# An encoder layer on one core: weight-block sums for w_o and four feed-forward groups moved from VectorE to accumulating DRAM transfers

## The chip, the cores and the metric

The kernel runs on one core of one Trainium2 chip. The metric is device time in microseconds of one execution. The kernel before took 1222.36 us, the median of three runs (1221.72 to 1222.45). One further execution was recorded by the hardware profiler; all trace times are counted from the start of its span.

## What is computed

One layer of an encoder, batch 1, 1024 positions, 1024 channels, fp32 throughout. The reference, cut to what matters here:

```python
mod = jax.nn.silu(c) @ w_ada + b_ada
sh1, sc1, gt1, sh2, sc2, gt2 = jnp.split(mod[:, None, :], N_MOD, axis=-1)

h = rmsnorm(x, norm1_g) * (1.0 + sc1) + sh1
z = h @ w_in
u, v, q, k, va, gate_a, gate_b = jnp.split(z, cuts, axis=-1)
a_out = gmlp_branch(u, v, gm_v_g, gm_w_s, gm_b_s) @ w_a
b_out = window_attention_branch(q, k, va, q_norm_g, k_norm_g, attn_sink) @ w_b
merged = jax.nn.sigmoid(gate_a) * a_out + jax.nn.sigmoid(gate_b) * b_out
x = x + gt1 * (merged @ w_o)

h2 = rmsnorm(x, norm2_g) * (1.0 + sc2) + sh2
f_gate, f_up = jnp.split(h2 @ w_ffn_in, 2, axis=-1)
x = x + gt2 * ((jax.nn.silu(f_gate) * f_up) @ w_ffn_out)
```

`w_ffn_in` is split into `w_gate` and `w_up`, 1024 x 2816 each, handled in 22 groups of 128 columns.

## The kernel before

**Precision.** Every fp32 operand is split into a high part (a copy to float32r) and a low part (operand minus high part). A product is three matrix multiplications: high x high, high x low, low x high. The high part is made on ScalarE (ACT), the low part mostly on VectorE (DVE), so each weight tile of 128 x 1024 costs one ACT copy and one DVE subtraction before TensorE (PE) may use it.

**Stages.** The positions are handled in two halves of 512. For each half: q, k, v, windowed attention and the gating branch, two branch projections. Then, over all 1024 positions, the gates (`gate_products`), the output projection (`out_products`), the feed-forward up and gate projections, and the down projection.

**Seven products instead of eight.** From the gates on, a product over two halves of the positions and two blocks of weight rows is done as a 2 x 2 block product by Winograd's scheme: seven block products, with sums of weight blocks and of activation blocks in place of the eighth. With weight blocks a11, a12, a21, a22 the sums are

- w1 = a21 + a22
- S = a11 + w1
- al = a12 + S
- w2 = a11 + a21

In a feed-forward group f, a11 and a12 are the two 512-column halves of `w_gate[f]`, a21 and a22 those of `w_up[f]`. Four *units* of weights are split for each group: unit 0 is the raw gate block, unit 1 is S beside w1, unit 2 is al beside w2, unit 3 is a22 alone. `STEPS` lists the seven products by unit, half and activation block. For w_o, the blocks of pair p are the halves of `w_o[2p]` and `w_o[2p+1]`, four pairs in all.

**Where the sums are made.** For w_o: during attention of the second half, `merged_sums` loads a pair into one `mid` tile (two loads of 512 KB on SyncE's queue, SP), four DVE additions make the sums in place, and one store of 1 MB on GpSimd's queue (POOL) writes them to the DRAM tile `sO`. `out_products` later loads parts of `sO` into `raw` tiles (`need`, kinds A and C). For the feed-forward groups: `prep(f, u, part)` does them while PE works; for unit 1 and for unit 2 two DVE sums each fill the tile `ws`, then part 0 makes the high part and part 1 the low part. In the kernel before, unit 1 holds -S, and the activation block T2 that it meets is plain.

**Order.** PE, ACT and DVE run in program order, written out by hand in the gates and in the feed-forward part (`in_order`, `manual_schedule`); `out_products` is ordered by a small planner, `Plan`, from costs and due times. SP issues nearly all loads, in order, and a load that waits for its buffer holds back those behind it. POOL issues the stores: `md` and `pd` (branch products, for the gates), `x1d` (the residual rows after w_o, read back by SP a little later), `tA`, `tB`, `wS`. POOL also computes the inverse square roots (`rcol`), which PE waits for through `spread`.

**The gates.** `gate_products` runs over six groups d = 2 to 7, each 84 multiplications of 128x512. Within a group: after the first product `gate_sums(d, 2)` makes sums on DVE and then issues the load of `gb` for group d + 1; after the fourth product `gate_sums(d + 1, 1)` reads it. At the end of a group `load_p` loads the four `pd` tiles of the next. In the first group, after its sixth product, two loads of `md` (512 KB each) are issued on POOL.

**Buffers.** `raw` and the split weights `wh`, `wl` have three buffers each, `mid` eight. The feed-forward part loads a gate block three groups ahead (`load_gate`), an up block two groups ahead (`load_up`, two buffers), and the fourth block of group 0 by itself into the `ss` tile. `run_chain` works off the list of activation blocks (`t1_sum`, `t2_sum`, `low`, ...) beside the first products; each entry is one or two instructions.

Of the kernel before, what the change touches and what calls it, by code (L numbers as in the profile page):

```python
# [16 lines left out]
P = 128  # L17
# [17 lines left out]
FA, FB, FC = 2, 1, 4  # L35
PLAIN_GATES = 2
ZEROS = (9, 1)
BIAS = 4
# [69 lines left out]
def kernel(  # L108
# [209 lines left out]
    tB = dram.tile([NP, P, 4 * HALF], F32, tag="tB", name="tB")  # L318
    sO = dram.tile([KT // 2, P, 4 * HALF], F32, tag="sO", name="sO")


# [251 lines left out]
    def open_ffn():  # L573
# [3 lines left out]
        fps.append(fp)  # L577

    def merged_sums(p):

        t = mid.tile([P, 2048], F32, tag="mid", name=nm("wo"))
        for i in range(2):
            load(t[:, i * UNIT : (i + 1) * UNIT], w_o[2 * p + i])
        a11, a12, a21, a22 = (t[:, i * HALF : (i + 1) * HALF] for i in range(4))
        ops = [(a22, a21, a22), (a21, a11, a21), (a11, a22, a11), (a12, a11, a12)]

        def one(n):
            out, a, b = ops[n]
            V.tensor_tensor(out, a, b, op=ALU.add)
            if n == 3:  # L590
                store(sO[p], t)
        return one

# [49 lines left out]
    def half(hf):  # L643
# [416 lines left out]

        pts = None
        pair_sums = [merged_sums(0)] if hf else []
        adds = 0
        for s in range(nw):
# [5 lines left out]
            if hf == 0:  # L1070
                if s % 2 == 0:
                    ada_load()
                if s:
                    ada_late(*ada_loaded.pop(0), silu_c)
                if s == nw - 1:
                    ada_late(*ada_loaded.pop(0), silu_c)
            else:
                if s % 2 == 0 and s < nw - 2:
                    pair_sums.append(merged_sums(s // 2 + 1))
                for _ in range((0, 3, 3, 2, 2, 2, 2, 2)[s]):  # L1080
                    pair_sums[adds // 4](adds % 4)
                    adds += 1
            fill(FA)
# [76 lines left out]
        for d in range(KT):  # L1160
# [24 lines left out]
            for j, (o, br) in enumerate(((512, (oH, oL)), (0, (gH, gL)))):  # L1185
# [9 lines left out]
                if d < PLAIN_GATES:  # L1195
                    sg = sgs.pop(0)
                    V.scalar_tensor_tensor(out=sg, in0=sg, scalar=1.0, in1=pb, op0=ALU.add, op1=ALU.mult)
                    ms.append(sg)
                else:
                    p = tmp()  # L1200
                    A.copy(p, pb)
                    store(pd[hf, d, 1 - j], p)
            if d < PLAIN_GATES:
# [181 lines left out]
    def gate_products(hH, hL):  # L1385
# [14 lines left out]
        def merge(s, p):  # L1400
            V.scalar_tensor_tensor(out=s, in0=s, scalar=1.0, in1=p, op0=ALU.add, op1=ALU.mult)

        run_tokens(99)
        tokens.extend(tokens_late)
        run_tokens(4)
        ps = load_p(GD[0])
        for d in GD:
            banks = {}
            for i, (u, part, t, b, first) in enumerate(STEPS):
# [382 lines left out]

    RG, RU, U = {}, {}, {}
    a22 = []

# [11 lines left out]
    def load_up(f):  # L1807
        if f < NF:
            RU[f] = ups[f % 2]
            dma(RU[f], w_up[f])  # L1810

    def prep(f, u, part):

        g, r = RG[f], RU.get(f)
        if part == 0:
            if u == 1:
                V.tensor_tensor(ws[:, Q:], r[:, :Q], r[:, Q:], op=ALU.add)
                V.scalar_tensor_tensor(out=ws[:, :Q], in0=ws[:, Q:], scalar=-1.0, in1=g[:, :Q],
                                       op0=ALU.mult, op1=ALU.subtract)
            elif u == 2:  # L1820
                V.tensor_tensor(ws[:, Q:], g[:, :Q], r[:, :Q], op=ALU.add)
                V.tensor_tensor(ws[:, :Q], g[:, Q:], ws[:, :Q], op=ALU.subtract)
            U[f, u] = wtiles(UNIT if u < 3 else Q)
            A.copy(U[f, u][0], (g, ws, ws, a22[0] if f == 0 else r[:, Q:])[u])
            return
        h, l = U[f, u]
        V.tensor_tensor(l, (g, ws, ws, a22[0] if f == 0 else r[:, Q:])[u], h.bitcast(F32), op=ALU.subtract)
        if u == 2:
            load_gate(f + 3)
        if u == 3 and f or (f, u) == (0, 2):  # L1830
            load_up(f + 2)
# [123 lines left out]
    def chain_12(rb):  # L1955
        for k in range(4):
# [3 lines left out]
            if k:  # L1960
                chain.append(lambda k=k: low(X0[:, k - 1, :], T2, k - 1))
            chain.append(lambda k=k: low(X0[:, k, :], T1, k))
            chain.append(lambda k=k: t2_sum(k))
        chain.append(lambda: low(X0[:, 3, :], T2, 3))

# [81 lines left out]
    with tc.manual_schedule():  # L2047
        U[4, 0], U[5, 0], U[0, 0], U[1, 0] = early
        buf = mid.tile([P, 2048], F32, tag="mid", name=nm("ws"))
        ws, ups = buf[:, :UNIT], (buf[:, UNIT:], fp.tile([P, UNIT], F32, tag="ru", name="ru"))  # L2050
        load_up(0)
        load_up(1)
        g3 = gate_raw(3)
        load_gate(0)
        product(0, 0)
        U[2, 0] = wtiles()
        split2(raw2[0], *U[2, 0])
        evict(0, 0)
        load_gate(1)
        product(0, 1)  # L2060
# [259 lines left out]
```

## Time and profile before

| what | us |
|---|---|
| median of three runs | 1222.36 |
| the profiled execution | 1221.94 |
| its span, first to last instruction | 1220.2 |
| PE busy | 1211.0 |
| DVE busy | 928.5 |
| ACT busy | 582.4 |
| POOL busy | 150.6 |

The granted TensorE clock is full throughout (1.00). Attention of the second half lies around 270 to 345 us of the span, the gates around 387 to 501, the output projection around 501 to 575, and the first feed-forward groups follow.

A row of the page's groups reads: line, engine, operation, out<-in by the program's names, shapes, count, then busy us, mean ns of one, idle time of the engine just before and what ended it. Nearly all compute instructions are recorded through one helper and carry its line, L145, so the tile names tell them apart. A row of the timeline reads: start us, duration, engine, line, operation, tiles, count, and in brackets the idle time before it and its releaser. A row of transfers gives count, KB of each and the median us from issue to landing. The view of waits reads: who waited for whom, us in total, times, longest. SPq is the issuing of transfers by SyncE.

### The profile page before, as it was taken

What the parts mean: (1) busy time and instruction counts of PE and PEld (TensorE: products, weight loads), DVE (VectorE), ACT (ScalarE), POOL (GpSimd) and SP (SyncE); (2) the same over time, 40 slices, a digit from 0 to 9 for tenths busy, and PEclk for the clock granted to TensorE, in tenths of its full rate; (3) what the DMA queues carried; (4) which work ended last, traced back from release to release, by engine and by line L of the source; (5) the groups of instructions that cost most, each with busy time, mean ns of one, the idle gap of its engine ahead of it and who ended that gap; (6) DMA issues with size and microseconds to landing.
All of it is one profiled execution on the core that took longest, in us unless ns stands there. A gap on an engine that the chain in (4) does not pass through costs nothing.

```text
span 1220.2 us, 15626 instructions
## 1 busy us (share of the span) xinstructions
PE 1211.0 (99%) x5653; PEld 1007.2 (83%) x5653; DVE 928.5 (76%) x1504; ACT 582.4 (48%) x954; POOL 150.6 (12%) x182
## 2 busy tenths in 40 slices
PE   9999999999999999999999999999999999999998
PEld 7888888888888888877888888888888888888887
DVE  8999977789978776897997767675676766765646
ACT  5667865367855443644553333333333334433341
POOL 0024323024322000001100001000000000000001
PEclk9999999999999999999999999999999999999999
DMA  9752169653277233477313446455555449995552
GB/s 363 284 180 99 35 217 358 248 216 134 104 259 240 96 117 103 148 233 266 103 49 122 172 157 223 173 192 187 190 190 199 163 155 372 394 354 190 190 172 104
DMA packets 78096, 236.54 MB, mean 194 GB/s; under 512 B 8898, under 2 KB 9154, under 8 KB 72772
## 3 DMA queue, kind: packets, MB, share of 16 engines
q1 hardware_dynamic: 63028, 163.20, 38.6%
q0 software_dynamic: 14992, 72.36, 15.8%
q8 instruction: 44, 0.72, 0.3%
q14 instruction: 32, 0.26, 0.1%
HBM read 176.28 MB, written 59.24 MB: 193 GB/s over the span
## 4 chain that ended last, share of the span: by engine, by line
PE 93%; DVE 4%; issue 1%; DMA 1%; ACT 1%; POOL 0%; SPq 0%; DVEq 0%; ACTq 0%; POOLq 0%
PE mm L145 47%; PE at L145 46%; DVE mid L145 2%; DMA raw<-in_w_q_dram 1%; DVE wl L145 1%; DMA mid<-in_xA_dram 0%; DVE ss L145 0%; DVE h L145 0%; DVE ws L145 0%; ACT wh L145 0%; DVE t L145 0%; DVE tt1l L145 0%; ACT mid L145 0%; ACT h L145 0%; DVE b22l L145 0%
## 5 line engine op out<-in xcount | busy, mean ns | idle before, releaser
L145 DVE TENSOR_TENSOR wl<-raw,wh 128x1024 fp32r<-128x1024 f32 (+1 forms) x135 | 159.0, 1182 | 61.7 <-ACT wh L145 61.1
L145 ACT CAST wh<-raw 128x1024 fp32r<-128x1024 f32 (+1 forms) x149 | 152.2, 1023 | 112.1 <-PE mm L145 39.9
L145 PE MATMUL mm<-mid,wh 128*128 128x512 f32 x640 | 197.7, 390 | 0.8 <-DVE mid L145 0.8
L145 PEld LDWEIGHTS mm<-mid,wh 128*128 128x128 f32 x640 | 119.8, 188 | 25.8 <-DVE mid L145 1.2
L145 PE MATMUL mm<-wh,h 128*128 128x512 f32 x384 | 124.7, 397 | 0.5 <-ACT h L145 0.5
L145 PE MATMUL mm<-mid,wl 128*128 128x512 f32 x320 | 124.7, 390 | 0.0
L145 PE MATMUL mm<-h,wh 128*128 128x512 f32 x304 | 94.4, 392 | 0.0
L145 PE MATMUL at<-h,wh 128*128 128x512 f32 x304 | 93.9, 390 | 0.0
L145 PEld LDWEIGHTS mm<-wh,h 128*128 128x128 f32 x384 | 70.8, 188 | 14.2 <-ACT h L145 0.9
L145 DVE TENSOR_TENSOR wl<-ws,wh 128x1024 fp32r<-128x1024 f32 (+1 forms) x54 | 60.8, 1125 | 24.2 <-ACT wh L145 24.1
L145 ACT CAST wh<-ws 128x1024 fp32r<-128x1024 f32 (+1 forms) x54 | 52.5, 973 | 42.9 <-DVE ws L145 28.0
L145 PE MATMUL mm<-wl,h 128*128 128x512 f32 x192 | 71.2, 391 | 0.0
L145 PEld LDWEIGHTS mm<-mid,wl 128*128 128x128 f32 x320 | 60.1, 188 | 12.6
L145 PEld LDWEIGHTS at<-h,wh 128*128 128x128 f32 x304 | 56.9, 188 | 11.7
L145 PEld LDWEIGHTS mm<-h,wh 128*128 128x128 f32 x304 | 56.6, 188 | 11.6
L145 ACT ACTIVATE t<-t 128x512 f32<-128x512 f32 x46 | 28.4, 631 | 71.2 <-DVE t L145 71.2
L145 DVE TENSOR_TENSOR ol<-raw,oh 128x1024 fp32r<-128x1024 f32 x30 | 36.6, 1224 | 31.4 <-ACT oh L145 29.8
L145 PE MATMUL mm<-h,wl 128*128 128x512 f32 x152 | 59.4, 391 | 0.0
L145 PE MATMUL at<-h,wl 128*128 128x512 f32 x152 | 59.3, 390 | 0.0
L145 ACT ACTIVATE xs<-xs 128x512 f32<-128x512 f32 x21 | 13.3, 632 | 94.5 <-DVE xs L145 94.5
L145 ACT CAST oh<-raw 128x1024 fp32r<-128x1024 f32 x30 | 31.6, 1053 | 44.8 <-PE at L145 21.5
L145 PE MATMUL at<-wl,wh 128*128 128x512 f32 (+1 forms) x136 | 52.7, 388 | 0.0
(296 smaller groups left out, 2882.0 us busy)
## 6 DMA issues: line engine op xcount, KB each, us to landing
mid<-in_w_ada_dram SPq DMA_DIRECT2D x28, 512.0 KB, 8.3
raw<-in_w_gate_dram SPq DMA_DIRECT2D x28, 512.0 KB, 3.7
tA<-hid POOLq DMA_DIRECT2D x11, 1024.0 KB, 4.4
tB<-hid POOLq DMA_DIRECT2D x11, 1024.0 KB, 5.0
wo<-in_w_out_dram POOLq DMA_DIRECT2D x22, 512.0 KB, 5.9
wS<-wo POOLq DMA_DIRECT2D x11, 1024.0 KB, 5.2
raw<-wS SPq DMA_DIRECT2D x44, 256.0 KB, 3.4
raw<-tB SPq DMA_DIRECT2D x44, 256.0 KB, 5.2
```

The source lines that it names most:

```text
L145: ins = f(*args, **kw)
```

## The change

1. `merged_sums` and its calls in attention go. So do its eight loads, sixteen DVE sums and four stores.
2. A new DRAM tile `sF` holds S, w1, al, w2 of feed-forward groups 0 to 3 (`READY = 4`).
3. `all_sums`, called at the start of `gate_products`, issues 32 transfers on POOL's queue, DRAM to DRAM, 512 KB each. Sixteen copy a block to its place, sixteen add a block (or a sum) to what is there (`accum_op=ALU.add`). They are four chunks of four steps: w_o pairs 0 and 1, groups 0 and 1, w_o pairs 2 and 3, groups 2 and 3; a chunk starts two steps after the one before. Each add waits for the landing of the copy or the add that it builds on. They are tied behind the last `pd` store in issue order (`last_store`).
4. The two loads of `md` move from POOL's queue to SP's.
5. For groups 0 to 3 `prep` no longer sums: each unit is loaded ready-made into a `raw` buffer (`load_unit`; units 1 and 2 from `sF`, 512 KB, unit 3 from `w_up`, 256 KB), three units ahead. The up blocks are first loaded whole for group 4. The separate load of group 0's fourth block goes.
6. S is now positive, so T2 is negated where it is split: `t2_sum` copies with scale -1, and `t2_low` takes the place of `low` for it. For groups from 4 on the two-operation sums become plain ones.

Counted by engine, PE's instructions and their order are the same in both programs. DVE has 32 sums fewer. The adds and the multiplications' operands are otherwise the same.

```diff
+READY = 4
...
+    sF = dram.tile([READY, P, 4 * HALF], F32, tag="sF", name="sF")
+    last_store = [None]
+
+    def sum_dma(dst, src, **kw):
+        last_store[0] = after(nc.gpsimd.dma_start(dst, src, **kw), last_store[0])
+
+    def add_dma(dst, src):
+        sum_dma(dst, src, accum_op=ALU.add)
+
+    def sum_steps(dst, a11, a12, a21, a22):
+
+        S, w1, al, w2 = dst
+
+        return [lambda: (sum_dma(w1, a21), sum_dma(S, a11)),
+                lambda: (add_dma(w1, a22), sum_dma(w2, a11)),
+                lambda: (add_dma(S, w1), sum_dma(al, a12)),
+                lambda: (add_dma(w2, a21), add_dma(al, S))]
+
+    def quarters(t, f0, f1):
+        return [t[f0:f1, :, i * HALF : (i + 1) * HALF].rearrange("f p q -> p f q") for i in range(t.shape[2] // HALF)]
+
+    def ffn_sums(f0, f1):
+        return sum_steps(quarters(sF, f0, f1), *quarters(w_gate, f0, f1), *quarters(w_up, f0, f1))
+
+    def wo_sums(p0, p1):
+        w = [w_o.rearrange("(a b) p q -> b p a q", b=2)[i] for i in range(2)]
+        a = [w[i][:, p0:p1, j * HALF : (j + 1) * HALF] for i in range(2) for j in range(2)]
+        S, al, w2, w1 = quarters(sO, p0, p1)
+        return sum_steps((S, w1, al, w2), *a)
+
+    def all_sums():
+        chunks = [wo_sums(0, 2), ffn_sums(0, 2), wo_sums(2, 4), ffn_sums(2, 4)]
+        for n in range(2 * len(chunks) + 2):
+            for i, c in enumerate(chunks):
+                if 0 <= n - 2 * i < 4:
+                    c[n - 2 * i]()
...
-    def merged_sums(p):
-
-        t = mid.tile([P, 2048], F32, tag="mid", name=nm("wo"))
-        for i in range(2):
-            load(t[:, i * UNIT : (i + 1) * UNIT], w_o[2 * p + i])
-        a11, a12, a21, a22 = (t[:, i * HALF : (i + 1) * HALF] for i in range(4))
-        ops = [(a22, a21, a22), (a21, a11, a21), (a11, a22, a11), (a12, a11, a12)]
...
-            else:
-                if s % 2 == 0 and s < nw - 2:
-                    pair_sums.append(merged_sums(s // 2 + 1))
-                for _ in range((0, 3, 3, 2, 2, 2, 2, 2)[s]):
-                    pair_sums[adds // 4](adds % 4)
-                    adds += 1
...
-                    store(pd[hf, d, 1 - j], p)
+                    last_store[0] = nc.gpsimd.dma_start(pd[hf, d, 1 - j], p)
...
+        all_sums()
         run_tokens(99)
...
-                        pool_dma(merged[hf][0][:, :PLAIN_GATES, :],
+                        dma(merged[hf][0][:, :PLAIN_GATES, :],
                                  md[hf].rearrange("(a p) t -> p a t", p=P))
...
+    def load_unit(n):
+        f, u = order[n]
+        if f < READY:
+            R[n] = wpool.tile([P, UNIT], F32, tag="raw", name=nm("raw"))
+            if u < 3:
+                dma(R[n], sF[f][:, (u - 1) * UNIT : u * UNIT])
+            else:
+                dma(R[n][:, :Q], w_up[f][:, Q:])
+        else:
+            load_gate(f + u - 1)
+
     def prep(f, u, part):
 
+        if f < READY:
+            n, w = place[f, u], slice(0, UNIT if u < 3 else Q)
+            if part == 0:
+                U[f, u] = wtiles(w.stop)
+                A.copy(U[f, u][0], R[n][:, w])
+            else:
+                split_low(R[n][:, w], *U[f, u])
+                load_unit(n + 3)
+            return
...
-                V.scalar_tensor_tensor(out=ws[:, :Q], in0=ws[:, Q:], scalar=-1.0, in1=g[:, :Q],
-                                       op0=ALU.mult, op1=ALU.subtract)
+                V.tensor_tensor(ws[:, :Q], ws[:, Q:], g[:, :Q], op=ALU.add)
...
-        A.copy(T2[0][:, k, :], X0[:, k, :])
+        A.activation(T2[0][:, k, :], X0[:, k, :], AF.Identity, scale=-1.0)
+
+    def t2_low(k):
+        V.scalar_tensor_tensor(out=T2[1][:, k, :], in0=X0[:, k, :], scalar=-1.0,
+                               in1=T2[0][:, k, :].bitcast(F32), op0=ALU.mult, op1=ALU.subtract)
...
-        load_up(0)
-        load_up(1)
+        load_up(READY)
+        load_up(READY + 1)
         g3 = gate_raw(3)
-        load_gate(0)
+        load_unit(0)
...
-        load_gate(1)
+        load_unit(1)
...
-        load_gate(2)
+        load_unit(2)
...
-        a22.append(ss_tile()[:, :Q])
-        dma(a22[0], w_up[0][:, Q:])
```

More of the change, by code (lines that the diff above doesn't have):

```diff
@@ L577, in open_ffn @@
         fps.append(fp)
-    def merged_sums(p):
-        t = mid.tile([P, 2048], F32, tag="mid", name=nm("wo"))
-        for i in range(2):
-            load(t[:, i * UNIT : (i + 1) * UNIT], w_o[2 * p + i])
-        a11, a12, a21, a22 = (t[:, i * HALF : (i + 1) * HALF] for i in range(4))
-        ops = [(a22, a21, a22), (a21, a11, a21), (a11, a22, a11), (a12, a11, a12)]
[L587 to L592, printed above, removed]
     halo_v = {}
@@ L1061, in half @@
         pts = None
-        pair_sums = [merged_sums(0)] if hf else []
-        adds = 0
         for s in range(nw):
@@ L1790 @@
     T1, T2 = ((fpt(f"{n}h"), fpt(f"{n}l")) for n in ("tt1", "b22"))
-    RG, RU, U = {}, {}, {}
-    a22 = []
+    RG, RU, U, R = {}, {}, {}, {}
     def gate_raw(f):
@@ L1817, in prep @@
                 V.tensor_tensor(ws[:, Q:], r[:, :Q], r[:, Q:], op=ALU.add)
-                V.scalar_tensor_tensor(out=ws[:, :Q], in0=ws[:, Q:], scalar=-1.0, in1=g[:, :Q],
-                                       op0=ALU.mult, op1=ALU.subtract)
+                V.tensor_tensor(ws[:, :Q], ws[:, Q:], g[:, :Q], op=ALU.add)
             elif u == 2:
                 V.tensor_tensor(ws[:, Q:], g[:, :Q], r[:, :Q], op=ALU.add)
-                V.tensor_tensor(ws[:, :Q], g[:, Q:], ws[:, :Q], op=ALU.subtract)
+                V.tensor_tensor(ws[:, :Q], g[:, Q:], ws[:, :Q], op=ALU.add)
             U[f, u] = wtiles(UNIT if u < 3 else Q)
-            A.copy(U[f, u][0], (g, ws, ws, a22[0] if f == 0 else r[:, Q:])[u])
+            A.copy(U[f, u][0], (g, ws, ws, r[:, Q:])[u])
             return
         h, l = U[f, u]
-        V.tensor_tensor(l, (g, ws, ws, a22[0] if f == 0 else r[:, Q:])[u], h.bitcast(F32), op=ALU.subtract)
+        V.tensor_tensor(l, (g, ws, ws, r[:, Q:])[u], h.bitcast(F32), op=ALU.subtract)
         if u == 2:
             load_gate(f + 3)
-        if u == 3 and f or (f, u) == (0, 2):
+        if u == 3:
             load_up(f + 2)
@@ L1960, in chain_12 @@
             if k:
-                chain.append(lambda k=k: low(X0[:, k - 1, :], T2, k - 1))
+                chain.append(lambda k=k: t2_low(k - 1))
             chain.append(lambda k=k: low(X0[:, k, :], T1, k))
             chain.append(lambda k=k: t2_sum(k))
-        chain.append(lambda: low(X0[:, 3, :], T2, 3))
+        chain.append(lambda: t2_low(3))
     def chain_rest():
```

## The prediction

> **What bounds the kernel now.** I read the page first, its busy times and its chain, then what TensorE (PE) waited for, then the three stages that the change touches.
>
> ```profile
> PE 1211.0 (99%) x5653; PEld 1007.2 (83%) x5653; DVE 928.5 (76%) x1504; ACT 582.4 (48%) x954; POOL 150.6 (12%) x182
> ...
> PE 93%; DVE 4%; issue 1%; DMA 1%; ACT 1%; POOL 0%; SPq 0%; DVEq 0%; ACTq 0%; POOLq 0%
> ```
>
> PE is busy for 1211.0 of 1220.2 us and holds 93% of the chain that ended last. That is no share of a mixed program: it is one engine that never rests, so a change can only win what PE waits for. The list of those waits, for the whole span, is short:
>
> ```profile
> PE at L145 <- DVE identr L145: 1.9, 1, 1.9
> PE at L145 <- POOL rcol L145: 1.2, 1, 1.2
> PE mm L145 <- DVE mid L145: 0.8, 1, 0.8
> PE mm L145 <- ACT h L145: 0.5, 2, 0.3
> PE at L145 <- DVE ss L145: 0.3, 1, 0.3
> PE at L145 <- DVE mid L145: 0.3, 1, 0.3
> ```
>
> 5.0 us in all; 2.4 of it (identr, h) lie in the start, which isn't edited. The view of busy time by stretch says where PE idles: attention of the second half, gates, first feed-forward groups.
>
> ```profile
> 270.00:345.00 75.00, 74.96 (x403) 63.28 (x402) 69.85 (x177) 59.01 (x134) 28.90 (x20) 1.00 0.37 134
> 387.00:501.00 114.00, 114.00 (x505) 94.43 (x504) 81.12 (x112) 51.76 (x80) 2.53 (x4) 1.00 0.38 121
> ...
> 575.00:640.00 65.00, 64.69 (x292) 53.00 (x291) 61.33 (x91) 37.06 (x57) 4.28 (x7) 1.00 0.27 93
> 640.00:700.00 60.00, 60.00 (x267) 49.68 (x266) 43.34 (x61) 19.34 (x27) 2.20 (x4) 1.00 0.43 150
> ```
>
> The columns are PE, PEld, DVE, ACT, POOL busy us (instructions), granted clock, DMA share, GB/s. In attention DVE is 93% busy (69.85 of 75) and looks like a bound, yet PE idles 0.04 us there. In the gates PE issues 505 matmuls in 114.00 us, 0.226 us each, without a gap. The change alters no matmul: PE's order is the same in both programs.
>
> **The change, part by part.**
>
> *Work taken from DVE.* Sixteen sums for w_o in attention, and for four feed-forward groups four sums each, the first six of them before 617 us:
>
> ```profile
> L145 DVE TENSOR_TENSOR wo<-wo 128x512 f32<-128x512 f32 x16 | 10.9, 687 | 0.3
> ...
> L145 DVE TENSOR_TENSOR ws<-raw,ws 128x512 f32<-128x512 f32 x9 | 5.9, 685 | 0.0
> L145 DVE SCALAR_TENSOR_TENSOR ws<-ws,raw 128x512 f32<-128x512 f32 x6 | 4.2, 692 | 0.2
> ```
>
> That is 16 x 0.687 = 11.0 us and 16 x 0.687 = 11.0 us of DVE. The first 11.0 lie beside a PE that idles 0.04 us: worth at most 0.04. The eight loads of w_o (512 KB) and four stores to sO (1 MB) leave SP's and POOL's queues in the same stage, which PE doesn't see either. Of the second 11.0 one wait can be paid back:
>
> ```profile
> 613.85 0.68 DVE L145 TENSOR_TENSOR ws<-ru 128x512 f32<-128x512 f32 x1
> 614.57 0.69 DVE L145 SCALAR_TENSOR_TENSOR ws<-ws,raw 128x512 f32<-128x512 f32 x1
> ...
> 615.77 0.74 DVE L145 SCALAR_TENSOR_TENSOR mid<-mid,mod,at 128x512 f32<-128x512 f32 x1
> ...
> 616.66 1.62 PE L145 MATMUL at<-h,first 128*128 128x512 f32 x6 [0.31 <-DVE mid L145]
> ```
>
> PE waits 0.31 us for a bank that the last scaled row (615.77) still reads; two sums of 0.68 and 0.69 stand right ahead of it and go, and four more before them. So the 0.31 goes. Nothing is late next: the list shows no further wait up to 700 us. Gain 0.3; bounds 0 and 0.35.
>
> *Signs.* T2 is negated where it is split: four copies on ACT become activations, four plain subtractions on DVE a two-operation form.
>
> ```profile
> L145 ACT CAST b22h<-mid 128x512 fp32r<-128x512 f32 x4 | 2.5, 621 | 7.7 <-DVE mid L145 7.7
> ...
> L145 ACT ACTIVATE t<-t 128x512 f32<-128x512 f32 x46 | 28.4, 631 | 71.2 <-DVE t L145 71.2
> ```
>
> Nearest rows: 631 against 621 ns on ACT, 692 (the two-operation sum above) against 685 on DVE. Four times 10 and four times 7 ns stand in a chain of steps that loses 4.1 us of sums (6 x 0.69): nothing. From group 4 on a two-operation sum becomes a plain one, 7 ns cheaper and off the path.
>
> *The 32 transfers.* They stand on POOL's queue behind the last pd store and ahead of the first x1d store; nothing else of POOL lies between, since the two md loads move to SP.
>
> ```profile
> 389.61 0.54 POOL L204 DMA_DIRECT2D pd<-t  x1 [1.69 <-ACT t L145]
> 390.14 1.46 POOL L1257 DMA_DIRECT2D mid<-md  x2
> ...
> 541.87 0.56 POOL L204 DMA_DIRECT2D x1d<-xs  x1 [150.27 <-DVE xs L145]
> ```
>
> So the sums start at 390.2. Each is 512 KB; an issue of this shape (128x2x512) takes POOL 0.73 us (1.46 for two). Half copy, half add into DRAM. The row of transfers waits on itself: followed along POOL's order, the adds that must land one after the other are nine (w1 and S of each of the four chunks, al of the last), behind one copy. With P for a copy, A for an add and 3 us for issues that stand in between, the last sum lands P + 9A + 3 after the start, POOL is free after P + 8A + 3, pairs 0 and 1 of sO are whole after about P + 3A + 2, pairs 2 and 3 after P + 7A + 3. No add into DRAM is in this trace. Nearest rows:
>
> ```profile
> raw<-in_w_gb_dram SPq DMA_DIRECT2D x10, 512.0 KB, 3.7
> ...
> mid<-hd SPq DMA_DIRECT2D x4, 1024.0 KB, 8.5
> ...
> hd<-mid SPq DMA_DIRECT2D x1, 1024.0 KB, 14.9
> ...
> mid<-md POOLq DMA_DIRECT2D x2, 512.0 KB, 6.6
> ```
>
> P is the row of the same shape and queue, 6.6. A lies between 3.7 (512 KB, the quickest) and 14.9 (the slowest of 1 MB, and it writes DRAM). An add of 512 KB reads two operands, so 1 MB, from DRAM: I take the 1 MB read, 8.5. Then pairs 0 and 1 are whole at 390.2 + 6.6 + 25.5 + 2 = 424.3, pairs 2 and 3 at 459.3, POOL is free at 467.8, the last sum lands at 476.3. They are wanted here:
>
> ```profile
> 508.35 3.70 SPq L199 DMA_DIRECT2D raw<-sO  x4
> ...
> 529.87 1.85 SPq L199 DMA_DIRECT2D raw<-sO  x4
> ...
> 575.72 20.06 SPq L1260 DMA_DIRECT2D raw<-in_w_gate_dram  x4
> ```
>
> Spare: 84 us for the first sO load, 70 for the second, 74 for x1d on POOL at 541.87, 99 for sF, whose loads take the place of the gate loads from 575.72 on. Its upper bound, A at 14.9: the last sum lands at 533.9 and POOL is free at 519.0: still ahead of all four. At 3.7 all is done by 433. So the cover holds over both bounds; it is gone when 8A exceeds 541.87 - 390.2 - 9.6 = 142.1, at A = 17.8.
>
> The Trainium skill weighs this row otherwise ("Collectives: The Full Stack", the section on the bandwidth ceiling): an add in the transfer path is slow only because it has two source reads, which halves about 31 GB/s per engine. An estimate from that page: 16 engines at half of it carry 512 KB in 2.1 us, 1.1 more than a copy, so A would be 7.7 and the last sum would land at 469. No run here shows an add yet; both sums end in the cover.
>
> *md on SP.* Two issues of some 0.4 us come behind the ga load of group 3 and ahead of the next pd loads. POOL issued them at 390.14 without a wait, so their tiles are free before SP reaches them near 403: no stall, and 1 MB of reads moves 13 us later.
>
> *What the sums do to the gates' loads.* The dearest wait would be on gb, whose load leaves last before its use:
>
> ```profile
> 426.56 0.62 PE L145 MATMUL mm<-h,wh 128*128 128x512 f32 x2
> ...
> 430.60 0.33 SPq L199 DMA_DIRECT2D raw<-in_w_gb_dram  x1
> ...
> 436.67 0.69 DVE L145 TENSOR_TENSOR gsum<-raw 128x512 f32<-128x512 f32 x1
> ...
> 440.44 0.69 DVE L145 TENSOR_TENSOR t<-mm,t 128x512 f32<-128x512 f32 x1 [1.75 <-PE mm L145]
> 441.04 1.22 DVE L145 TENSOR_TENSOR wl<-raw,wh 128x1024 fp32r<-128x1024 f32 x1
> ```
>
> It leaves at 430.60 and lands 3.7 later, 2.4 ahead of gsum at 436.67. If gsum were late, DVE has 1.75 idle at 440.44 to catch up; the next group's low part ends at 442.26, and PE, whose group began at 426.56 and has 84 matmuls of 0.226 (19.0), wants it at 445.6. So gb may land 2.4 + 1.75 + 3.3 = 7.4 us later than now, 11.1 after its issue, before PE waits. How full do the engines get?
>
> ```profile
> DMA  9752169653277233477313446455555449995552
> GB/s 363 284 180 99 35 217 358 248 216 134 104 259 240 96 117 103 148 233 266 103 49 122 172 157 223 173 192 187 190 190 199 163 155 372 394 354 190 190 172 104
> ...
> raw<-in_w_q_dram SPq DMA_DIRECT2D x7, 512.0 KB, 9.4
> ```
>
> Sixteen copies of 0.52 MB and sixteen adds that read 1.05 are 25 MB; in 86 us that is 290 GB/s beside the stage's 121 (share 0.38). Together 411, over the fullest slice (394, share 9): the engines are full while the sums run. Held to 394 - 121 = 273 the sums take 92 us and end at 482, which changes nothing above. But gb then goes as 512 KB of w_q went, most of it in the full slices at the start: 9.4, not 3.7. It lands 1.7 before PE would wait. Cost 0; bounds 0 and, at the 14.9 above, 3.8 for each of the four or five groups that the sums cover: 17.
>
> *Feed-forward units.* Units of groups 0 to 3 come ready from sF through the three raw buffers, each loaded three units ahead, at least three products (8 us) before its split, against 3.7 for 512 KB: nothing.
>
> **Sum.** 1221.94 (the profiled execution, 1220.2 span and 1.7 around it) - 0.3 = 1221.6. That execution lies 0.4 below the median of the three runs (1222.36), so in medians: 1222.0. Own range: 1220.5 to 1224.
>
> **The rivals.**
>
> *Faster.* DVE's relief in attention feeds PE after all: short waits among its small matmuls, which the busy view hides. For: DVE is 93% busy there and gets 11.0 of 69.85 us back. Against: 0.04 us idle, no PE wait listed between 270 and 345. If 403 matmuls hid 2.5 us there, with the 0.3: 1219.5.
>
> *Slower, through sharing.* Place: gate groups 2 to 6, the gb load. It decides from 11.1 us after its issue. For: full engines, 9.4 as a median of seven, so some loads above it, and only 1.7 us of room behind that. Against: DVE's idle time and the room return with each group, so lateness doesn't add up. At 12.5 us, five times 1.4: 1229; at 14.9, + 17: 1239. The Trainium skill has a rule behind it ("DMA: Bandwidth & Descriptors", "Issuing engines are not separate DMA queues"): transfers that different engines start run on the same DMA engines and interleave, so a queue of its own on POOL doesn't shield SP's loads. By that rule alone gb, sharing with one full queue, would take an estimated twice 3.7, 7.4, and PE wouldn't wait; no run here shows the two together.
>
> *Slower, through the row itself.* An add takes more than 17.8 us: POOL is still in the sums at 541.87, the x1d stores and the power on POOL behind them, which PE waits for already (rcol, 1.2), come late. Price 8 x (A - 17.8): at 22, + 34, 1256. Against: slower than any row above. The sums then wouldn't be what they say, hidden.
>
> **Chances.** Forecast 0.60, faster rival 0.09, sharing 0.22, row 0.09. 0.2% of 1222.36 is 2.4 us, about what a measurement of this kernel can tell from no change: bounds 1219.9 and 1224.8. So faster 0.09, within 0.60, slower 0.31. The range leaves out the row (0.09), a fifth of sharing (0.04) and half of the faster case (0.05): 1219.5 to 1237.
>
> **What would show it.** Right: PE's waits in attention stay empty, the 0.31 at 616.66 is gone, the last sum lands near 476, sO is loaded at 508 with no wait on a sum, gsum in the gates never waits for raw. Wrong: PE idle in 387 to 501, SP or ACT waiting for sO or sF, POOL's first x1d behind 542, or an add row above 17.8.

## The result, and the profile after

The changed kernel takes 1229.3 us (median of 6 runs, 1228.10 to 1230.95), the kernel before beside it 1222.32 (6 runs, 1221.42 to 1223.31). The ratio is 1.0059, 95% interval 1.0046 to 1.0072: slower by 7.0 us, three times what counts here as no change. The forecast of 1222.0 did not come; the rival "slower, through sharing" did, at its place. The profiled execution took 1228.88 us, 1227.1 of it span.

The page of the changed kernel, its busy times, slices, and the engines of the chain that ended last:

```profile
PE 1212.3 (99%) x5653; PEld 1009.2 (82%) x5653; DVE 908.4 (74%) x1472; ACT 581.8 (47%) x954; POOL 176.7 (14%) x208
...
DMA  9742169621177999867414546455554439995552
GB/s 363 280 179 99 35 223 361 240 86 52 36 263 236 272 275 204 238 213 253 154 35 143 183 154 223 157 177 210 193 189 181 169 151 365 394 369 189 189 172 103
...
PE 88%; DMA 6%; DVE 4%; issue 1%; ACT 1%; SPq 0%; DVEq 0%; ACTq 0%
```

DVE lost 20.1 of its 928.5 us. But PE's share of the chain fell from 93% to 88, and DMA's rose from 1% to 6, half of it the load of gb; slices 14 to 16 (some 399 to 491 us, most of the gates) moved 272, 275 and 204 GB/s where before 96, 117 and 103 stood. What PE waited for in the changed kernel (us in total, times, longest):

```profile
PE mm L146 <- DVE t L146: 4.3, 2, 3.5
PE at L146 <- DVE ss L146: 1.9, 2, 1.6
PE at L146 <- DVE identr L146: 1.9, 1, 1.9
PE at L146 <- DMA mid<-in_w_ada_dram: 1.0, 1, 1.0
```

The first line is new, and all of it lies in the gates: waits of 0.89 and 3.45 us. Both programs issue the same 5653 matmuls in the same order, so the start of one and the same matmul can be compared across traces. From these starts comes this table: us that each profiled execution spent between six fixed matmuls (those that the kernel before starts at 270, 387, 500, 545, 575 and 640 us). The first two rows are the kernel before, twice; the other names are the experiments of the next section.

```
                start  attention  gates  w_o, first  w_o, last  ffn 0-3   rest     span
                       2nd half          part        part
before         270.02     117.11 112.88      45.18      29.93    64.99  580.05  1220.16
b2_before      270.00     117.09 112.88      45.21      31.31    64.96  579.65  1221.09
after          270.88     115.75 119.71      45.80      31.39    64.21  579.35  1227.10
e1_copies      270.78     115.79 121.04      45.99      29.74    64.21  579.40  1226.94
e2_ready2      270.72     115.79 117.88      45.83      31.17    64.19  579.04  1224.61
e5_paced       269.92     115.78 114.87      45.61      31.58    64.17  579.04  1220.96
e8_worst       269.81     115.79 113.83      45.39      29.77    64.21  578.99  1217.77
e10_three      270.08     115.78 115.19      45.41      30.22    64.16  579.02  1219.85
e6_two         269.91     115.78 112.88      45.19      29.56    64.15  579.02  1216.50
e9_two4        270.63     115.79 112.88      47.33      29.71    64.21  579.36  1219.90
e7_paced4      269.31     115.75 113.45      47.53      30.55    64.19  579.57  1220.35
e13_nogb       269.71     115.79 113.08      45.02      32.00    64.16  579.32  1219.09
e4_attention   293.99     116.79 112.88      45.37      29.49    64.21  579.39  1242.13
e12_noadds     270.38     115.79 112.88      45.91      31.40    64.98  579.23  1220.57
```

Read the row "after" against "before": the gates cost 6.83 us more, attention 1.36 less, the first feed-forward groups 0.78 less. The first part of w_o costs 0.62 more, but that can't be laid to the change: e12_noadds, which is the kernel before in that stage, shows 0.73 more, and in both traces PE waits 0.5 us for `xs` there. The start (+0.86), the last part of w_o (+1.46) and the rest (-0.70) differ between executions of kernels that are alike in those stages, as the columns show.

How the gates lose it: SP's, DVE's and PE's order of time in the changed kernel, where the longer of the two waits stands.

```profile
470.88 0.33 SPq L200 DMA_DIRECT2D raw<-in_w_gb_dram  x1
...
477.80 0.69 DVE L146 SCALAR_TENSOR_TENSOR t<-t,xs 128x512 f32<-128x512 f32 x1 [4.00 <-DMA xs<-pd]
478.41 0.69 DVE L146 TENSOR_TENSOR wl<-raw,wh 128x512 fp32r<-128x512 f32 x1
483.50 0.69 DVE L146 TENSOR_TENSOR gsum<-raw 128x512 f32<-128x512 f32 x1 [4.40 <-DMA raw<-in_w_gb_dram]
484.22 0.69 DVE L146 SCALAR_TENSOR_TENSOR gsum<-gsum,raw 128x512 f32<-128x512 f32 x1
484.83 0.68 DVE L146 TENSOR_TENSOR t<-mm,t 128x512 f32<-128x512 f32 x1
...
485.57 0.73 PE L146 MATMUL mm<-mid,wh 128*128 128x512 f32 x2 [3.45 <-DVE t L146]
```

gb leaves at 470.88 and DVE gets it at 483.50. Behind gsum on DVE stands `t<-mm,t`, which reads the bank that the last product of the group (`mm<-mid,wh`) adds into. So PE stands 3.45 us. The loss goes on after the wait; busy times by stretch of 2 us, in which the seventh quantity (behind the length and PE, PEld, DVE, ACT, POOL) is the granted clock:

```profile
485.00:487.00 2.00, 1.43 (x6) 1.21 (x7) 2.00 (x3) 0.63 (x1) 0.00 (x0) 1.00 0.99 101
487.00:489.00 2.00, 2.00 (x6) 1.55 (x6) 1.30 (x3) 1.12 (x2) 0.00 (x0) 0.51 1.04 196
489.00:491.00 2.00, 2.00 (x7) 1.56 (x7) 1.97 (x3) 1.05 (x2) 0.00 (x0) 0.64 0.95 182
491.00:493.00 2.00, 2.00 (x11) 1.65 (x10) 1.97 (x5) 0.06 (x1) 0.63 (x1) 1.00 0.80 305
```

A clock of 0.51 and 0.64 for 2 us each costs 0.98 + 0.72 = 1.7 us: the trace has the half clock on record for 3.41 us. The gates' 6.83 are then 4.3 of waits, 1.7 of clock, and 0.8 that lies mostly in the matmuls next to the two waits.

And how late the transfers were, by kind, from 387 to 506 us (count, KB each, median us from issue to landing):

```profile
sO<-in_w_o_dram POOLq DMA_DIRECT2D x12, 512.0 KB, 12.2
...
raw<-in_w_gb_dram SPq DMA_DIRECT2D x5, 512.0 KB, 9.9
hs<-pd SPq DMA_DIRECT2D x10, 256.0 KB, 7.5
xs<-pd SPq DMA_DIRECT2D x10, 256.0 KB, 8.9
...
sO<-sO POOLq DMA_DIRECT2D x4, 512.0 KB, 10.8
```

### The profile page after: what moved, and what is told of

Its sections match the earlier page's. It is cut to its first block, busy times and chain, and to the rows that moved or that the text cites. A ratio compares the mean times of both kernels' runs of the same rounds, so it can differ in the third digit from the quotient of the medians.

```text
span 1227.1 us, 15618 instructions
## 1 busy us (share of the span) xinstructions
PE 1212.3 (99%) x5653; PEld 1009.2 (82%) x5653; DVE 908.4 (74%) x1472; ACT 581.8 (47%) x954; POOL 176.7 (14%) x208
## 4 chain that ended last, share of the span: by engine, by line
PE 88%; DMA 6%; DVE 4%; issue 1%; ACT 1%; SPq 0%; DVEq 0%; ACTq 0%
PE at L146 45%; PE mm L146 43%; DMA raw<-in_w_gb_dram 3%; DVE t L146 1%; DVE wl L146 1%; DVE mid L146 1%; DMA mid<-in_w_ada_dram 1%; DMA raw<-in_w_q_dram 1%; DMA raw<-in_w_ada_dram 1%; DMA mid<-in_xA_dram 1%; DVE gsum L146 0%; DMA raw<-sO 0%; DVE raw L146 0%; ACT wh L146 0%; DVE ss L146 0%
## 5 line engine op out<-in xcount | busy, mean ns | idle before, releaser
L146 DVE TENSOR_TENSOR wl<-raw,wh 128x1024 fp32r<-128x1024 f32 (+1 forms) x147 | 171.3, 1169 | 66.2 <-ACT wh L146 61.8
L146 ACT CAST wh<-raw 128x1024 fp32r<-128x1024 f32 (+1 forms) x161 | 163.0, 1014 | 116.9 <-PE mm L146 41.4
L146 DVE TENSOR_TENSOR wl<-ws,wh 128x1024 fp32r<-128x1024 f32 (+1 forms) x45 | 50.3, 1117 | 22.3 <-ACT wh L146 22.3
L146 PEld LDWEIGHTS mm<-h,wh 128*128 128x128 f32 x304 | 56.9, 189 | 11.7
L146 PEld LDWEIGHTS at<-h,wh 128*128 128x128 f32 x304 | 56.9, 188 | 11.7
L146 ACT CAST wh<-ws 128x1024 fp32r<-128x1024 f32 (+1 forms) x45 | 43.5, 967 | 31.2 <-DVE ws L146 18.8
```

Source lines behind the costliest of these rows:

```text
L146: ins = f(*args, **kw)
```

## The experiments

**Is it the add's second read?** All adds become plain copies; the sums are left out.

```diff
     def add_dma(dst, src):
-        sum_dma(dst, src, accum_op=ALU.add)
+        sum_dma(dst, src)
```

> The sixteen adds become plain copies to the same places, with the same waits between them; so the sums of w_o and of feed-forward groups 0 to 3 are left out (each place keeps the block copied last). Sharing (the sums' traffic delays the gb loads of the gates): a copy reads one operand instead of two, the transfers get shorter than the 8 to 14 us of the changed kernel, gb lands within 9 us of its issue, PE idles under 1 us between 387 and 501, time 1221 to 1224. Rival, the moved md loads and the order of SP's queue: nothing of that changes, gb stays at 10 to 12 us, 1228 to 1230. Rival, mere number of DRAM-to-DRAM transfers: gb at 9.5 to 12 as before, 1227 to 1230.

1229.35 us (4 runs), ratio 1.0058 (1.0044 to 1.0071): as slow as the change. Its gb and one kind of its copies, from 405 to 480 us:

```profile
raw<-in_w_gb_dram SPq DMA_DIRECT2D x4, 512.0 KB, 11.6
...
sF<-sF POOLq DMA_DIRECT2D x4, 512.0 KB, 6.0
```

The copies land sooner (sF<-sF 6.0 us, against 9.7 for the adds in the changed kernel), and the last lands at 478 instead of 513 us. But four, four and three of them are in flight when the first gb loads leave, and gb is no earlier. The loss doesn't need the adds' second reads; plain transfers are enough for it. That leaves the other two explanations, the order on SP and the mere transfers, and e4 below tells them apart.

**Fewer sums.** Two feed-forward groups instead of four: 24 transfers.

```diff
-READY = 4
+READY = 2
...
-        chunks = [wo_sums(0, 2), ffn_sums(0, 2), wo_sums(2, 4), ffn_sums(2, 4)]
+        chunks = [wo_sums(0, 2), ffn_sums(0, 2), wo_sums(2, 4)]
```

> Sums for feed-forward groups 0 and 1 only (24 transfers instead of 32). Sharing: the row of transfers ends some 25 us sooner, near 485, so the gb load that leaves near 471 meets less traffic; the 3.45 us wait of PE at 481.7 and the half clock behind it (1.6) shrink or go, the 0.9 at 423 stays: 1223 to 1226. Rival, md and SP's order: 1228 to 1230. Rival, the row of sums reaches into the output projection and costs there: 1226 to 1228, with the wait at 481 unchanged.

1223.60 us (10 runs), 1.0013 (1.0003 to 1.0022). The second long wait is gone; the one at the first gb, which leaves into the same opening burst, stays. It is even longer, gb 12.5 us after its issue and PE 3.11 us idle where the changed kernel had 10.3 and 0.89. Up to there both kernels issue the same transfers, so that is a difference between executions, and this one (1226.38) is the slowest of e2's ten.

**Elsewhere.** The sums one round per block of attention, on POOL in program order; the md loads stay on SP.

```diff
+            all_sums(8 * hf + s, 8 * hf + s + 1)
...
-        all_sums()
```

> All 32 transfers kept, issued on POOL one step (2 to 4 transfers) at the end of each attention block: eight steps in the first half, two in the second; md stays on SP. Sharing in the gates is the cause: the gates have no PE wait (gb lands 3.5 to 4.5 after issue), the small gains of the changed kernel remain (attention of the second half about 1.3, first feed-forward groups about 0.7): 1220 to 1222. Rival, md and SP's order in the gates: the waits at 423 and 482 stay, 1228 to 1230. Rival, POOL held up by the waits of the sums (or loads delayed) inside attention: PE waits there, gates clean, 1224 to 1235.

1243.93 us (5 runs), 1.0181 (1.0167 to 1.0195). The gates take 112.88 us as before, so the md loads on SP are innocent, and the sums do the harm in the gates. But the start takes 293.99 instead of 270.02. POOL works for attention there, and an add of the row makes it wait (order of time on POOL, 120 to 145 us):

```profile
135.43 1.14 POOL L325 DMA_DIRECT2D sF<-sF  x1 [7.17 <-DMA sF<-in_w_up_dram]
136.15 1.14 POOL L325 DMA_DIRECT2D sF<-in_w_gate_dram  x1
136.87 1.81 POOL L325 DMA_DIRECT2D sO<-in_w_o_dram  x2
138.73 1.04 POOL L146 CAST kbuf<-kbuf 128x1024 fp32r<-128x1024 f32 x1
```

The cast waits behind 7.17 us of waiting and 3.3 of issues. The chain that ended last shows that it matters: from 107.6 to 161.9 us it goes through four landings of the row, of 11.7, 15.4, 10.2 and 11.6 us. Loads suffer too: xB's two loads of 1 MB take 14.5 us from 60 to 260 us, 7.1 before. How the 24 us divide between the two stays open.

**Is gb the load that counts?** DVE waits 4.00 us for xs<-pd as well. So gb of groups 3 to 7 isn't loaded: ga's block stands in, and these gates are computed from other data.

```diff
-            gb_raw[d] = raw_unit(w_gb[d])
+            gb_raw[d] = ga_raw[d] if d > PLAIN_GATES else raw_unit(w_gb[d])
```

> The change with all its sums, unlimited, but the gb blocks of gate groups 3 to 7 aren't loaded: ga's block stands in for them, so the sums in these groups are of other data. If gb's lateness is what PE waits for: no wait of PE over 0.3 us between 390 and 500 us, some 6.9 us less than the change, 1221.5 to 1223.5 us. If the pd loads of the merges, for which DVE waited 3.7 and 4.0 us, are late enough by themselves: waits of 2 us or more stay, 1225 us and more.

1219.94 us (10 runs), 0.9980 (0.9971 to 0.9989): 9.4 us less than the change, where some 6.9 were expected; where the other 2.5 come from stays open. All that PE waited for in that kernel:

```profile
PE at L146 <- DVE ss L146: 2.2, 1, 2.2
PE at L146 <- DVE identr L146: 1.9, 1, 1.9
PE mm L146 <- DVE mid L146: 0.8, 1, 0.8
PE mm L146 <- ACT h L146: 0.3, 2, 0.2
```

No line of it lies in the gates (113.08 us), though all 32 sums run there as in the change, and the pd loads are as late: from 405 to 480 us 9.2 us for xs and 8.4 for hs, against 9.0 and 7.7 in the changed kernel. Late pd loads alone cost PE nothing; gb does.

**When, or how many at once?** Four kernels. In the first two the 24 transfers go in rounds of two or four; from the third round on, each is held until the bank of a group's fourth product (e5) or first product (e8) is copied on ACT.

```diff
         last_store[0] = after(nc.gpsimd.dma_start(dst, src, **kw), last_store[0])
+        if pace[0] is not None:
+            tc.add_manual_dep(
+                last_store[0].ins, pace[0].ins.name,
...
-                    A.copy(c22, bank)
+                    pace[0] = A.copy(c22, bank)
+                    n = 2 + list(GD).index(d)
+                    all_sums(n, n + 1)
```

> The sums of w_o and of two feed-forward groups (24 transfers), each round of 2 or 4 transfers held until the fourth product's bank is copied, that is until the group's gb load has landed. If the lateness of gb comes from leaving into a burst of 4 or 5 transfers in flight: every gb load takes under 5 us, PE has no wait over 0.5 us between 390 and 500 us, 1221.0 to 1222.5 us. If it is the sums' volume in the stage, wherever it lies: gb at 6 to 12 us in most groups, a wait of PE in the gates of 2 to 4 us, 1223 to 1226 us.

> The same 24 transfers in the same rounds, held until the first product's bank is copied instead, some 1 us before gb leaves. If it is the burst that gb leaves into: gb at 9 to 12.5 us behind each round of four transfers, waits of PE on DVE in two to five groups, 1226 to 1232 us. If it is the volume: the same as with rounds behind the fourth product, within 1 us.

In the third no transfer starts before the one two ahead of it has landed; the fourth does the same with three.

```diff
+        if len(flight) > 1:
+            tc.add_manual_dep(
+                last_store[0].ins, flight[-2].ins.name,
...
+        flight.append(last_store[0])
```

> The same 24 transfers, each held until the one two before it has landed, so that no more than two are in flight. If gb's time follows from the number in flight: 5 to 8.5 us in every group until the last sum lands (460 to 500 us), under the 9.4 or so from which PE waits, so no wait of PE in the gates over 0.5 us, 1221.0 to 1222.8 us. If any sum beside gb is enough: 9 us and more, waits in two or more groups, 1224 to 1230 us.

> 24 transfers, each held until the one three before it has landed. If gb's time grows with the number in flight (two: 6.0 to 6.7 us): 7 to 9 us, no wait of PE in the gates over 0.5 us, 1218 to 1220 us. If three already fill the engines as the whole row does: one gb at 9.6 us or more, a wait of PE over 0.8 us, 1221 us and more.

| kernel | runs | median us | ratio to before (95%) | profiled run, us | its gates, us | its gb, us from issue to landing |
|---|---|---|---|---|---|---|
| e5, behind the 4th product | 11 | 1220.63 | 0.9984 (0.9975 to 0.9993) | 1222.74 | 114.87 | 10.4, 7.6, 10.7 |
| e8, behind the 1st product | 12 | 1223.10 | 1.0001 (0.9992 to 1.0010) | 1219.55 | 113.83 | 10.0, 4.1, 4.0 |
| e10, three in flight | 11 | 1221.22 | 0.9988 (0.9979 to 0.9998) | 1221.62 | 115.19 | 9.8, 9.6, 9.7 |
| e6, two in flight | 6 | 1218.63 | 0.9973 (0.9962 to 0.9984) | 1218.28 | 112.88 | 6.4, 6.0, 6.7 |

Both expectations on rounds missed in their mechanism. A round of four takes 16 to 20 us from its first issue to its last landing, so in e5 a round begun after gb is still in flight when the next gb leaves. In e8 a round of four that is let go just ahead of gb turned out harmless; transfers of it and gb's, from 448 to 450 us:

```profile
sF<-in_w_up_dram POOLq DMA_DIRECT2D x1, 512.0 KB, 9.4
raw<-in_w_gb_dram SPq DMA_DIRECT2D x1, 512.0 KB, 4.1
sF<-sF POOLq DMA_DIRECT2D x1, 512.0 KB, 12.2
```

The round's first transfer left 0.2 us ahead of gb, the other three behind it, and gb took 4.1 us; it was the transfers that were slow (9.4 and 12.2 us). (That execution is e8's quickest, 3.5 us under its median; what the others lose stays open.) With three in flight the rival came true in gb's time, 9.6 to 9.8 us, though PE's waits were 0.45, 0.29 and 0.67 us and none over 0.8. Two in flight did what was expected of it, gb at 6.0 to 6.7; the time is 2.4 us under the expected range, and only part of that is accounted for: of 4.2 us under the kernel before, the table of stages places 1.32 in attention and 0.84 in the first feed-forward groups, and the rest stays open. In these traces gb's time goes with what is in flight when it leaves. Counted over 13 traces (all but e13) from the issue and landing of each transfer; each trace has four gb loads behind the start of the sums, one of them without a landing record:

```
sums in flight    gb loads    us from issue to landing
when gb leaves
      0              12            3.4 to 4.2
      1               4            4.0 to 6.4
      2               6            6.0 to 7.3
      3               9            7.6 to 11.6
      4               4            9.6 to 11.8
      5               4           10.0 to 12.5
```

The number doesn't fix the time alone: with three in flight it spans 4 us. How far each transfer ahead is from its landing, and what leaves behind gb, weren't varied by themselves.

The amount moved doesn't decide. Busy times from 387 to 501 us of e2, of e6 and of e13, in that order (the last quantity is GB/s, the first busy time PE's):

```profile
387.00:501.00 114.00, 110.89 (x483) 91.36 (x482) 76.51 (x108) 48.73 (x75) 23.12 (x26) 0.99 0.85 226
```

```profile
387.00:501.00 114.00, 114.00 (x504) 94.42 (x504) 81.04 (x114) 52.85 (x80) 22.81 (x25) 1.00 0.87 229
```

```profile
387.00:501.00 114.00, 114.00 (x504) 94.13 (x503) 80.32 (x113) 52.60 (x80) 30.28 (x33) 1.00 0.94 235
```

e2 and e6 move the same 24 transfers at 226 and 229 GB/s; with no limit PE loses 3.1 us in the profiled execution, with two in flight nothing. In medians e2 lies 1.3 us above the kernel before beside it, and e6 4.2 below (1222.86, 30 runs). So e6 beats both kernels.

**All 32 transfers, done so.** e9 is the change with two in flight; e7 has its rounds behind the fourth product.

> The change as it is, all 32 transfers, but each held until the one two before it has landed. If the number in flight is what the change costs: gb in the gates at 5.5 to 7.5 us, no wait of PE there over 0.5 us, the last sum lands near 520 us (32 transfers at the 4.1 us each that 24 took), 1217.5 to 1219.5 us. If the late sums of groups 2 and 3 cost the output projection what the gates are spared: a wait on ss of 1.4 us or more with some eight matmuls of 427 ns behind it, 1220 to 1223 us.

> All 32 transfers (four feed-forward groups) in rounds behind the fourth product; the last two rounds fall behind the gates. If the gates' gb load is all that the change costs: 1221.0 to 1222.5 us, PE's waits in the gates empty. If the output projection pays as well, its sO loads beside the late rounds: gates empty, but a wait of PE between 520 and 575 us of 1.5 us or more and some rows at half clock behind it, 1223 to 1226 us.

e9: 1223.94 us (11 runs), 1.0006 (0.9997 to 1.0014). e7: 1223.42 (11 runs), 1.0005 (0.9994 to 1.0015). Both expected the gates clean, and they nearly are (112.88, and 113.45 with one wait of 0.23). Both pay in the first part of w_o instead, 2.15 and 2.35 us over before, but not by the wait on ss that was expected. Some 0.5 of it is the wait on `xs` that e12 shows too. For the rest, the last sum lands at 531 us in e9, and PE waits for blocks of w_o whose loads share with the row (first row ACT, which waits for such a load):

```profile
515.27 1.05 ACT L146 CAST wh<-raw 128x1024 fp32r<-128x1024 f32 x1 [2.30 <-DMA raw<-in_w_o_dram]
...
516.37 0.73 PE L146 MATMUL mm<-h,wh 128*128 128x512 f32 x2 [0.52 <-ACT wh L146]
517.63 0.50 PE L146 MATMUL mm<-h,wl 128*128 128x512 f32 x1 [0.53 <-DVE wl L146]
```

The profiled execution of e9 (1221.67) lies 2.3 us under its median; where the others lose that stays open.

**Where do the gains come from?** The kernel before without its sixteen sums on DVE; sO then holds the bare blocks of w_o.

```diff
             out, a, b = ops[n]
-            V.tensor_tensor(out, a, b, op=ALU.add)
```

> The kernel before without its sixteen sums for w_o on DVE in attention: loads and stores stay, so sO holds the bare blocks. If DVE's relief there is what the change gains: 1.0 to 1.5 us less than before. If it is the loads and the stores that go with them, or nothing: within 0.4 us of before.

1220.99 us (12 runs), 0.9988 (0.9980 to 0.9997): 1.9 less than the 1222.87 of before beside it, 0.4 to 2.4 by the interval. Attention takes 115.79 us, as in every kernel that makes the sums in DRAM outside it, with w_o's loads and stores still there. The gain in attention, 1.32 us, is DVE's relief.

**Is the last part of w_o the change's work?** The kernel before, profiled again.

> The kernel before, unchanged, profiled a second time, for the output projection alone: there the change showed a wait of PE on ss of 1.58 us with some eight matmuls of 427 ns behind it, the kernel before 0.31 us on ss and 1.17 on rcol at full clock. If the longer wait is the change's work: 0.2 to 0.5 us on ss again, and about 1.2 on rcol. If it differs from one execution to the next whatever the sums do (the kernel before without its additions showed 1.59 us and half clock too): any value from 0.3 to 2.2 us on ss, and matmuls of 427 ns behind it where it is over 1.38 us.

1222.88 us (one run). Its PE at the place in question, and the stretch behind:

```profile
562.93 1.05 PE L145 MATMUL at<-ones,ss 128*128 128x1 f32 x8 [1.51 <-DVE ss L145]
...
565.27 0.63 PE L145 MATMUL mm<-tt1h,wl 128*128 128x512 f32 x1
565.70 0.63 PE L145 MATMUL mm<-tt1h,wh 128*128 128x512 f32 x1
...
565.00:567.00 2.00, 2.00 (x7) 1.54 (x6) 1.38 (x3) 0.53 (x1) 1.20 (x2) 0.50 0.95 352
```

The unchanged kernel shows the same wait and the half clock. It is no part of the change, though it makes single executions differ by 1.4 us.

## Why the prediction was wrong, point by point

**The step that failed: "What the sums do to the gates' loads", cost 0.** Three things in it.

*The time of gb.* It took 9.4 us from w_q's row. Measured: 9.6 to 12.5 in the changed kernel, 10.3 in the middle. What I reasoned from, a full DMA, is no measure: at a DMA share of 0.87 gb takes 6.0 to 6.7 us in e6, at 0.85 it takes 6.4 to 12.5 in e2. The number to ask for was how many transfers are ahead of gb; the 32, which wait only for their operands, put five, four and five ahead of the three gb loads whose landing is on record.

*The room.* 11.1 us was taken, from the next group's low part as the first that PE would miss. PE waits earlier, for `t<-mm,t`, which stands among the rows shown there and was passed over. When the last product of the group wants its bank, in the kernel before:

```profile
442.66 0.39 PE L145 MATMUL at<-b22h,wl 128*128 128x512 f32 x1
442.88 0.62 PE L145 MATMUL mm<-mid,wh 128*128 128x512 f32 x2
```

`t<-mm,t` ended at 440.44 + 0.69 = 441.13, 1.75 ahead of 442.88. This gb itself landed 3.5 us after its issue, 2.6 ahead of gsum, so the room is 3.5 + 2.6 + 1.75 + 1.75 = 9.6 us. Some 0.2 of it goes in handing over: in the changed kernel gsum starts 0.1 behind gb's landing, and PE 0.06 behind the end of `t<-mm,t`. So gb may take 9.4, not 11.1. The gb that leaves at 411 to 412 us confirms it: at 9.8, 10.3, 10.4, 11.8 and 12.5 us (e10, after, e5, e1, e2) PE waits 0.45, 0.89, 1.02, 2.44 and 3.11, each time the excess over 9.4 within 0.1. Later gb loads don't keep to it: 10.7 us cost 0.37 in e5 and 10.0 nothing in e7, and why stays open. With 9.4 as room and 9.4 as time, the likeliest case had no margin, and a chance of 0.22 for the rival was too low.

*What a wait costs.* In the prediction a wait cost its own length; the 1.7 us at reduced clock behind the wait of 3.45 us were in no case.

**The rival "slower, through sharing".** Place and sign were right. Its 1229 at a gb of 12.5 us agrees with the 1229.3 by luck: the sum is another, two waits of 0.9 and 3.5 and the clock, less the gains below, instead of five times 1.4. That lateness would not add up was right: between the two waits the gates recover. With the rule of the Trainium skill that transfers started by different engines run on the same DMA engines and interleave ("DMA: Bandwidth & Descriptors", "Issuing engines are not separate DMA queues") the traces agree: transfers from POOL's queue delay SP's loads. The estimate of 7.4 drawn from it holds for two sums in flight (6.0 to 7.3), not for five (10.0 to 12.5).

**Work taken from DVE: "worth at most 0.04".** It was worth 1.32 (e12) to 1.36, the faster rival's mechanism at about half its price. The rows that would have shown it are waits of PEld, the weight load, and only PE's waits were read. From 270 to 345 us the kernel before has three of them, in both its traces; the changed kernel and e12 have none:

```profile
PEld at L145 <- DVE nmx L145: 0.4, 1, 0.4
PEld at L145 <- DVE lb L145: 0.4, 1, 0.4
PEld at L145 <- DVE xs L145: 0.3, 1, 0.3
```

The one for lb, in order of time, in the kernel before:

```profile
324.80 1.40 DVE L145 TENSOR_TENSOR wo<-wo 128x512 f32<-128x512 f32 x2
...
326.94 1.57 PE L145 MATMUL at<-ident,lb 128*128 128x128 f32 x8
...
326.94 1.33 PEld L145 LDWEIGHTS at<-ident,lb 128*128 128x128 f32 x8 [0.35 <-DVE lb L145]
```

And in the changed kernel:

```profile
326.99 1.04 PE L146 MATMUL at<-ident,lb 128*128 128x128 f32 x8
```

Two sums of w_o stand ahead of lb's scaling; the eight transposes that take lb as weights go through at DVE's pace, 1.57 us instead of 1.04, and count as busy. Matmul by matmul against e12, some 0.6 us of the 1.32 are lost here, and as much at the other two, at 287 to 289 us. Idle time of 0.04 was thus no bound.

**The 0.31 at 616.66** went, as forecast; the stage gained 0.78, of which the rest is near that place (the matmul ahead and the ones at 622) and was not costed.

**A, P and the row.** P at 6.6 was right for a copy alone: the first two copies took 6.3 and 6.7 us. A was 8.5. Told apart by the program's order, the sixteen adds took 7.8 to 18.1 us, 13.0 in the middle, and the sixteen copies 6.3 to 16.0, 12.5 in the middle: in the crowded row a copy is about as slow as an add. So the chain of nine adds behind one copy was not the path either: of the twelve landings that POOL waited for, eight were copies. The engines were full, as reckoned (share 0.95 from 387 to 501 us), but they moved 246 GB/s there, not 394. The last sum lands at 513, not 476 or 482.

The cover held all the same: no load of sO or sF waits for a sum, and "through the row itself" fell. Two signs of it came nevertheless. Two adds took 18.1 us, over the 17.8, but no transfer of the row waits for them; and POOL's first x1d store leaves at 548.85, but that is 7.0 us late as the gates are, 35 us behind the last sum. The Trainium skill's rule that an add's second read slows it ("Collectives: The Full Stack", the section on the bandwidth ceiling) agrees in direction: with copies in place of the adds the row took 88.6 us instead of 123.8. The size of it for one add was not separated from the crowding, and it does not decide: with copies the time of the kernel was the same.

**md on SP, the feed-forward units, the signs:** cost nothing, as forecast (the gates of e4, and the column of groups 0 to 3).

## What to carry to other kernels

Transfers that are "hidden" still stand in the way of the loads that have a due time: ask how many are in flight when such a load leaves, and cap that number; the same 24 transfers with two in flight instead of all that were ready turned 1223.6 us into 1218.6. Take a load's room from the first reader of anything queued behind it on its engine, up to the bank that TensorE adds into, not from its own reader alone. And read the waits of the weight loads as well: in attention TensorE was fed slowly and still counted as busy.

## What the hardware showed besides

Half clock after short waits. At the same place of the output projection, waits of PE of 1.39 (e2), 1.51 (b2), 1.58 (after), 1.59 (e12), 1.81 (e5) and 2.25 us (e13) were each followed, 0.6 to 2.4 us after they ended, by a few matmuls of 427 instead of 227 ns; 1.34 (e8), 1.38 (e1) and, against the series, 1.82 us (e10) were not. In the gates 2.44 (e1), 3.11 (e2) and 3.45 us (after) were followed by it, and 3.15 us (e1) was not. Each time the half clock stayed for 3.41 us by the traces' clock records, so it cost 1.7 us whatever the length of the wait. The Trainium skill ("TensorE: Matmul & The Clock Gate", "What's actually happening") puts an idle window of about 3.4 us that runs freely before the half clock; that much the same wait brings it or not agrees with a free-running window, that 1.39 us can be enough does not agree with the length.
